# Half-width products in a triangular inversion, and a last tile that leaves in three pieces

## The chip, the cores and the metric

The program runs on one core of a Trainium2 chip, in one launch. The metric is the time of one execution on the device in microseconds (us). The kernel before took 2224.36 us, the median of three runs.

## The reference

One inference step of a two-layer decoder trunk, for a prompt of 2048 tokens of width 1024 and for 8 short samples of 8 tokens. Layer 0 mixes tokens with a gated DeltaNet of 6 heads, layer 1 with a short gated convolution. Both layers have memory attention beside the mixer, a gate, an output projection and a residual add; a final RMSNorm ends the trunk. The change touches two places of it, the solve in the delta rule and the end:

```python
A = jnp.tril(jnp.einsum('bnhid,bnhjd->bnhij', kb, k) * decay, -1)
rhs = jnp.concatenate([kb * jnp.exp(G)[..., None], v * beta[..., None]], axis=-1)
wu = lax.linalg.triangular_solve(A + jnp.eye(C, dtype=A.dtype), rhs, left_side=True,
                                 lower=True, unit_diagonal=True)
...
x = x + br @ w_out[i].astype(x.dtype)
...
y = rmsnorm(x, final_norm_g)
```

## The kernel before

**The order of the work.** The kernel is written as many small generators ("jobs"). A planner, `Flow` (lines 143 to 230), runs them while it records the instructions: it keeps a clock for each engine from a table of costs and always goes on with the job of highest priority that is ready on PE's clock. The order of the instructions on each engine is what comes out of this, so a changed cost moves instructions everywhere behind it. On the chip every engine takes its instructions strictly in that order and waits on semaphores. `mm` (line 319) issues all matrix products, so they all show as L330; the vector, scalar and GpSimd instructions all show as L281.

**The tiles.** Activations lie as 4 tiles of 512 tokens, plus one tile of the 64 sample tokens. A projection of a tile by a weight block is 24 products: 8 blocks of the depth, three float16 partial products each, 512 columns wide (64 for the samples). They are named `psp<-ht,whl` in layer 0.

**The inversion.** In layer 0 each head and tile is an item with 4 chunks of 128 tokens (one of 64 for the samples). `wy_inv` (lines 1552 to 1636) inverts the unit lower triangular matrices of two chunks at a time, 128 by 128 each, by doubling: at level `li`, blocks of side `1 << li` are joined in pairs. It holds U, the transposed inverse so far, and L, both float16, in one buffer `UL` (profile name `ul`). A level has four steps:

- PE: `pq`, A16 by L, 2 products of 128 columns (one for each chunk).
- DVE: `qq`, `pq` times a mask of the level, 128x256 to float16.
- PE: `pu`, `qq` by U and U by `qq`, 4 products of 128 columns.
- ACT: one copy of all of `pu`, 128x512, back into `ul`.

There are 6 such levels (2 for the samples), 24 items with two inversions each, so 288 levels of the wide kind, and 12 of the narrow. At a level, though, only half of the columns of U and of L get new values; in `qq` the other half are columns of the identity. GpSimd (POOL) makes U's first value and the low part `Ml` of the matrix, and works at other things in the same phase: the gates' masks `gm`, the identity added in `dd`, `whl` (the low halves of the weights) and the powers `rk`, `rq` and `hr`. `qq`, `A16`, `Ml`, `gm` and `ee` share 12 buffers (`kqc`).

**The end.** In layer 1 `out_group` (lines 2052 to 2111) makes the output projection of the tiles in the order 0, 1, 2, samples, 3. Tile 3 is done in two units of 256 tokens. Each of a unit's 8 blocks loads its rows of the residual (`xo`), and `ev` adds the product to them on DVE. `final` (lines 2130 to 2144) takes the unit's RMSNorm through `row_scale` (line 644): squares on ACT, their sum over the 8 blocks one after the other on POOL, one product with ones (`rb`) on PE, a power on POOL, a second product that spreads the result over the partitions, and then for each block one DVE instruction, which writes `yt`, a buffer of 4, and one store.

Of the kernel before, what the change touches and what calls it, by code (L numbers as in the profile page):

```python
# [15 lines left out]
AF = mybir.ActivationFunctionType  # L16
ALU = mybir.AluOpType
# [4 lines left out]
P = 128  # L22
D = 1024
KB = 8
NT = 4
# [261 lines left out]
def hybrid_kernel(  # L287
# [107 lines left out]
    def gbank(name):  # L395
        return psum("bank", [P, 4, P], 8, name)
# [16 lines left out]
    def kq16(name):  # L413
        return gp.tile([P, 2, P], F16, tag="kq", name=name, bufs=NKQ)
# [322 lines left out]
    def half(name, w=UN):  # L737
        return k1(name).rearrange("p z f -> p (z f)")[:, :w]
# [661 lines left out]
    def rows(x, n, C):  # L1400
        return x[:n, :n].rearrange("p (o f) -> p o f", o=1).to_broadcast([n, C, n])
# [150 lines left out]
    def wy_inv(it, i):  # L1552

        n, hc = it.n, it.hc
        lv = 7 if n == P else 3
        yield from wait(it.M_ok[i])
        M = it.M[i]  # L1560
        G.tensor_tensor(M[:n, :hc, :n], M[:n, :hc, :n], rows(identKh, n, hc), op=ALU.add)
        yield
        yield from ulc.get()
        yield from kqc.get(2)
        A16 = kq16("A16")
        V.tensor_copy(A16[:n, :hc, :n], M[:n, :hc, :n])
        UL = gp.tile([P, 4, P], F16, tag="k1", name="ul", bufs=NK1)
        U, L = UL[:n, 0:2], UL[:n, 2:4]
        yield
        yield from gc_.get()  # L1570
        pq = gbank("pq")
        for z in range(hc):
            mm(pq[:n, z, :n], A16[:n, z, :n], identh[:n, :n])
        t = fl.cur.t
        G.tensor_tensor(U[:, :hc, :n], A16[:n, :hc, :n], rows(mask_u, n, hc), op=ALU.mult)
        fl.cur.t, fl.cur.eng = t, "PE"
        yield
        V.tensor_tensor(L[:, :hc, :n], pq[:n, :hc, :n], rows(masks[:, 0], n, hc), op=ALU.mult)
        gc_.put()
        yield  # L1580
        Ml = None
        for li in range(1, lv):
            yield from gc_.get()
            pq = gbank("pq")
            for z in range(hc):
                mm(pq[:n, z, :n], A16[:n, z, :n], L[:, z, :n])
            if Ml is None:
                t = fl.cur.t
                Ml = kq16("Ml")
                G.tensor_tensor(Ml[:n, :hc, :n], M[:n, :hc, :n], A16[:n, :hc, :n], op=ALU.subtract)  # L1590
                fl.cur.t, fl.cur.eng = t, "PE"
                Mc.put()
            yield
            yield from kqc.get()
            qq = kq16("qq")
            V.tensor_tensor(qq[:n, :hc, :n], pq[:n, :hc, :n], rows(masks[:, li], n, hc), op=ALU.mult)
            gc_.put()
            yield
            yield from gc_.get()
            pu = gbank("pu")  # L1600
            for z in range(hc):
                mm(pu[:n, z, :n], qq[:n, z, :n], U[:, z, :n])
            for z in range(hc):
                mm(pu[:n, 2 + z, :n], U[:, z, :n], qq[:n, z, :n])
            kqc.put()
            yield
            if hc == 2:
                A.activation(UL[:n, :, :n], pu[:n, :, :n], AF.Copy)
            else:
                A.activation(UL[:n, 0:4:2, :n], pu[:n, 0:4:2, :n], AF.Copy)  # L1610
            gc_.put()
            yield
        yield from gc_.get()
        pe = gbank("pe")
        for z in range(hc):
            mm(pe[:n, z, :n], A16[:n, z, :n], L[:, z, :n], start=True, stop=False)
            mm(pe[:n, z, :n], Ml[:n, z, :n], L[:, z, :n], start=False, stop=True)
        yield
        kqc.put(2)
        yield from kqc.get()  # L1620
        ee = kq16("ee")
        V.tensor_tensor(ee[:n, :hc, :n], rows(identKh, n, hc), pe[:n, :hc, :n], op=ALU.subtract)
        gc_.put()
        yield
        yield from uc.get()
        yield from gc_.get()
        pu = gbank("pu1")
        for z in range(hc):
            mm(pu[:n, z, :n], ee[:n, z, :n], U[:, z, :n])
        kqc.put()  # L1630
        yield
        it.u[i] = k1("u1")
        V.scalar_tensor_tensor(it.u[i][:n, :hc, :n], pu[:n, :hc, :n], 1.0 / MS, U[:, :hc, :n], op0=ALU.mult, op1=ALU.add)
        gc_.put()
        ulc.put()
        fl.set(it.u_ok[i])
# [415 lines left out]
    def out_group(l, src, src_s, consume):  # L2052
# [2 lines left out]
        units = [(t, slice(0, TOK if t < NT else NS)) for t in seqn]  # L2055
        if l == 1:
            i = seqn.index(NT - 1)
            units[i:i + 1] = [(NT - 1, slice(u * UN, (u + 1) * UN)) for u in range(2)]
        for i, (t, cs) in enumerate(units):
            N = cs.stop - cs.start  # L2060
            yield from wait(ready[l][t])
# [9 lines left out]
            for k in range(KB):  # L2071
                w = ws[k]
                yield from use(w)
                with fl.aside():
                    V.tensor_tensor(isc8[:, k:k + 1], w.inv, inv, op=ALU.mult)
                if N == TOK:
                    yield from pc.get()
                    xo = piece("xo")
                    landed = dma(xo, src[t, :, k])
                elif t < NT:  # L2080
                    yield from xhc.get()
                    xo = half("xo")
                    landed = dma(xo, src[t, :, k, cs])
                else:
                    xo = xos[:, k]
                xt.append(xo)
                yield from ppc.get()
                ps = pbank()
                yield from proj(ps[:, :N], w, hl[:, :, :, cs])
                if i + 1 == len(units):  # L2090
                    w.free()

                def ev(ps=ps, xo=xo, k=k, t=t, N=N, isc8=isc8, landed=landed, fs=fs):
                    yield until(landed)
                    V.scalar_tensor_tensor(xo, ps[:, :N], isc8[:, k:k + 1], xo, op0=ALU.mult, op1=ALU.add)
                    ppc.put()
                    fl.set(fs[k])
                    if t < NT and l == 0:
                        yield
                        dma(x1_sp[t, :, k], xo)  # L2100
                    yield 0

                fl.spawn(5, ev(), "xo")
# [25 lines left out]

    def final(t, cs, xt, fs):  # L2130
        N = cs.stop - cs.start
        rb = yield from row_scale(xt, fs, N, G, (tmpc0, tmp0))
        for k in range(KB):
            yield from tmpc.get()
            yt = tmp("yt", N)
            V.scalar_tensor_tensor(yt, xt[k], fg[:, k:k + 1], rb[:, :N], op0=ALU.mult, op1=ALU.mult)
            if t < NT:
                (pc if N == TOK else xhc).put()
            yield
            dma((y_o[t] if t < NT else ys_o)[:, k, cs], yt)  # L2140
            tmpc.put(1, 2500.0)
        gc_.put()
        if t == NT:
            pc.put()
# [158 lines left out]
```

## Time and profile before

| | |
|---|---|
| median of 3 runs | 2224.36 us (2221.85 to 2230.78) |
| the profiled execution, its own time | 2225.13 us |
| its span, first to last instruction | 2223.4 us |
| PE busy | 2147.2 us, 97% |
| DVE, ACT, POOL busy | 1488.9, 1120.7 and 714.3 us |
[...]

The busy time of PE counts each product from its start to the modelled end. Products are pipelined: the next one starts long before the one in front has ended. So what a product costs in a row of them is read from the distance of starts in the timeline, not from its own duration.

### The profile page before, as it was taken

What the parts mean: (1) busy time and instruction counts of PE and PEld (TensorE: products, weight loads), DVE (VectorE), ACT (ScalarE), POOL (GpSimd) and SP (SyncE); (2) the same over time, 40 slices, a digit from 0 to 9 for tenths busy, and PEclk for the clock granted to TensorE, in tenths of its full rate; (3) what the DMA queues carried; (4) which work ended last, traced back from release to release, by engine and by line L of the source; (5) the groups of instructions that cost most, each with busy time, mean ns of one, the idle gap of its engine ahead of it and who ended that gap; (6) DMA issues with size and microseconds to landing.
All of it is one profiled execution on the core that took longest, in us unless ns stands there. A gap on an engine that the chain in (4) does not pass through costs nothing.

```text
span 2223.4 us, 43011 instructions
## 1 busy us (share of the span) xinstructions
PE 2147.2 (97%) x16176; PEld 1298.0 (58%) x16176; DVE 1488.9 (67%) x4228; ACT 1120.7 (50%) x2952; POOL 714.3 (32%) x901
## 2 busy tenths in 40 slices
PE   6889989999999999999999999999999999999998
PEld 5467657667666666666555454455444456555457
DVE  6988887887889878777777566355342437675354
ACT  5757665566657656566566345134221226653221
POOL 5655334442434433433222335012110212201322
PEclk9989999999999999999999999999999999999999
DMA  4201020201122102002134443022010111223433
GB/s 134 64 13 37 16 49 9 55 30 27 39 70 41 50 6 46 31 6 69 56 102 143 142 152 114 15 68 80 31 54 10 53 49 58 69 72 129 129 112 118
DMA packets 113634, 141.50 MB, mean 64 GB/s; under 512 B 50193, under 2 KB 67857, under 8 KB 113425
## 3 DMA queue, kind: packets, MB, share of 16 engines
q1 hardware_dynamic: 113424, 138.75, 20.5%
q8 instruction: 127, 2.08, 0.4%
q14 instruction: 83, 0.67, 0.1%
HBM read 99.22 MB, written 39.49 MB: 62 GB/s over the span
## 4 chain that ended last, share of the span: by engine, by line
PE 58%; DVE 3%; ACT 1%; issue 1%; DMA 1%; POOL 0%; POOLq 0%; DVEq 0%; ACTq 0%
PE psp L330 49%; PE psA L330 2%; PE psc L334 1%; PE pu L330 1%; PE po L330 1%; PE psc L330 1%; PE rb L330 1%; DVE wmx L281 1%; PE pq L330 1%; PE pqk L330 0%; DVE amx L281 0%; PE pkk L330 0%; DMA wraw<-in_wo 0%; DVE apT L281 0%; PE po L334 0%
## 5 line engine op out<-in xcount | busy, mean ns | idle before, releaser
L330 PE MATMUL psp<-ht,whl 128*128 128x512 f16 x5376 | 1270.0, 380 | 0.0
L330 PEld LDWEIGHTS <-whl 128*128 128x128 f16 x9408 | 753.6, 98 | 650.1 <-issue 12.6
L281 POOL TENSOR_TENSOR whl<-wraw,whl 128x512 f16<-128x512 f32 x184 | 216.8, 1182 | 448.0 <-ACT whl L281 400.2
L330 PE MATMUL psp<-hl,whl 128*128 128x512 f16 (+1 forms) x1728 | 342.4, 357 | 0.0
L281 ACT ACTIVATE ul<-pu 128x512 f16<-128x512 f32 x300 | 168.3, 582 | 79.6 <-PE pu L330 76.8
L281 ACT ACTIVATE wraw<-wraw,wsc 128x512 f32<-128x512 f32 (+1 forms) x186 | 131.7, 712 | 76.3 <-DVE wsc L281 44.6
L281 DVE SCALAR_TENSOR_TENSOR cacc<-psp,cws,cacc 128x511 f32<-128x511 f32 (+2 forms) x216 | 159.4, 738 | 10.1 <-ACT cacc L281 9.8
L281 POOL TENSOR_TENSOR nsq<-nsq 128x512 f32<-128x512 f32 (+2 forms) x105 | 100.6, 960 | 194.3 <-ACT nsq L281 149.1
L281 DVE TENSOR_TENSOR qq<-pq,masks 128x256 f16<-128x256 f32 x300 | 118.0, 407 | 51.1 <-PE pq L330 49.2
L281 DVE TENSOR_REDUCE wmx<-wraw 128x1 f32<-128x1024 f32 (+1 forms) x93 | 111.5, 1201 | 31.6 <-DMA wraw<-in_wb 24.5
L281 ACT ACTIVATE wg<-psp,hisc 128x512 f32<-128x512 f32 x64 | 44.0, 687 | 171.6 <-PE psp L330 171.4
L281 ACT ACTIVATE nsq<-xo 128x512 f32<-128x512 f32 (+1 forms) x72 | 41.4, 580 | 150.8 <-DVE xo L281 86.8
L281 ACT ACTIVATE whl<-wraw 128x512 f16<-128x512 f32 x184 | 114.8, 626 | 2.7
L281 DVE SCALAR_TENSOR_TENSOR xo<-psp,isc,xo 128x512 f32<-128x512 f32 (+1 forms) x72 | 49.6, 688 | 95.2 <-PE psp L330 95.2
L281 DVE SCALAR_TENSOR_TENSOR wg<-wg,psp 128x512 f32<-128x512 f32 x64 | 43.6, 681 | 87.8 <-ACT wg L281 87.8
L330 PEld LDWEIGHTS <-A 128*128 128x128 f16 x792 | 69.4, 100 | 41.1 <-issue 10.4
L281 ACT ACTIVATE ape<-psc,amx,sa 128x256 f32<-128x256 f32 x128 | 70.8, 561 | 31.7 <-DVE amx L281 31.6
L330 PE MATMUL pu<-ul,qq 128*128 128x128 f16 (+1 forms) x588 | 81.8, 224 | 3.9 <-DVE qq L281 3.1
L330 PE MATMUL pq<-ul,A 128*128 128x128 f16 (+1 forms) x588 | 77.0, 224 | 4.6 <-ACT ul L281 2.6
L330 PE MATMUL pu<-qq,ul 128*128 128x128 f16 (+1 forms) x588 | 81.2, 223 | 0.0
L281 POOL TENSOR_TENSOR rk<-sse,mhalf 128x4 f32<-128x4 f32 (+1 forms) x30 | 27.6, 919 | 159.9 <-DVE sse L281 118.8
L281 DVE SCALAR_TENSOR_TENSOR raw<-psp,wisc,cg 128x512 f32<-128x512 f32 x24 | 18.0, 749 | 86.9 <-PE psp L330 86.8
(344 smaller groups left out, 3641.0 us busy)
## 6 DMA issues: line engine op xcount, KB each, us to landing
br_sp<-wg SPq DMA_DIRECT2D x64, 256.0 KB, 2.0
brl<-br_sp SPq DMA_DIRECT2D x64, 256.0 KB, 2.9
wraw<-in_wb SPq DMA_DIRECT2D x28, 512.0 KB, 3.5
wraw<-in_wa SPq DMA_DIRECT2D x24, 512.0 KB, 3.5
xk<-in_x SPq DMA_DIRECT2D x64, 128.0 KB, 2.9
wraw<-in_wo SPq DMA_DIRECT2D x16, 512.0 KB, 3.4
xo<-in_x SPq DMA_DIRECT2D x32, 256.0 KB, 3.5
x_sp<-xo SPq DMA_DIRECT2D x32, 256.0 KB, 2.4
```

The lines of the kernel that those rows point to most:

```text
L281: return f(out, *args, **kw)
L330: nc.tensor.matmul(out, lhsT=lhsT, rhs=rhs, start=start, stop=stop)
L334: nc.tensor.transpose(out, in_, ident)
```

## The change

In the inversion, the products of a level are made for the half of the columns that changes, 64 instead of 128 (32 instead of 64 for the samples); DVE masks half as many elements; ACT brings back the two halves in two instructions of 128x128, and the other halves of `ul` stay as they are. The half of `qq` that is a piece of the identity is written by a new POOL instruction (`unit`), ahead of the level: for the first one before the loop, for each later one right behind the `pu` products of the level before. The columns that change lie in runs of `1 << li` elements, with equal gaps.

At the end, tile 3 is done in units of 256, 128 and 128 tokens. The second and the third share the rows that are loaded for both. The last unit sums its squares with 8 products on PE instead of on POOL. `final` scales the rows in place and stores them from there; a row's buffer comes free 2.5 us (on the planner's clock) behind the store.

```diff
--- before.py
+++ after.py
@@ -1579,35 +1579,59 @@
         gc_.put()
         yield
         Ml = None
+
+        def halves(x, li):
+
+            v = x[:, :, :n].rearrange("p z (b h s) -> p z b h s", h=2, s=1 << li)
+            return v[:, :, :, 0], v[:, :, :, 1]
+
+        idh = identh[:n, :n].rearrange("p (o f) -> p o f", o=1)
+
+        def unit(li):
+
+            qq = kq16("qq")
+            i2 = halves(idh, li)[1].to_broadcast([n, hc, n >> (li + 1), 1 << li])
+            G.tensor_tensor(halves(qq[:n], li)[1][:, :hc], i2, i2, op=ALU.mult)
+            return qq
+
+        yield from kqc.get()
+        qq = unit(1)
+        fl.cur.t, fl.cur.eng = t, "PE"
         for li in range(1, lv):
+            nb = n >> (li + 1)
+            first, second = halves(L, li), halves(U, li)
+            qf = halves(qq[:n], li)[0]
             yield from gc_.get()
-            pq = gbank("pq")
+            pq = gbank("pq").rearrange("p c (b s) -> p c b s", s=1 << li)
             for z in range(hc):
-                mm(pq[:n, z, :n], A16[:n, z, :n], L[:, z, :n])
+                mm(pq[:n, z, :nb], A16[:n, z, :n], first[0][:, z])
+            t = fl.cur.t
             if Ml is None:
-                t = fl.cur.t
                 Ml = kq16("Ml")
                 G.tensor_tensor(Ml[:n, :hc, :n], M[:n, :hc, :n], A16[:n, :hc, :n], op=ALU.subtract)
-                fl.cur.t, fl.cur.eng = t, "PE"
                 Mc.put()
-            yield
-            yield from kqc.get()
-            qq = kq16("qq")
-            V.tensor_tensor(qq[:n, :hc, :n], pq[:n, :hc, :n], rows(masks[:, li], n, hc), op=ALU.mult)
+            fl.cur.t, fl.cur.eng = t, "PE"
+            yield
+            mask = halves(masks[:n, li:li + 1], li)[0].to_broadcast([n, hc, nb, 1 << li])
+            V.tensor_tensor(qf[:, :hc], pq[:n, :hc, :nb], mask, op=ALU.mult)
             gc_.put()
             yield
+
             yield from gc_.get()
-            pu = gbank("pu")
+            pu = gbank("pu").rearrange("p c (b s) -> p c b s", s=1 << li)
             for z in range(hc):
-                mm(pu[:n, z, :n], qq[:n, z, :n], U[:, z, :n])
+                mm(pu[:n, z, :nb], qq[:n, z, :n], second[1][:, z])
             for z in range(hc):
-                mm(pu[:n, 2 + z, :n], U[:, z, :n], qq[:n, z, :n])
+                mm(pu[:n, 2 + z, :nb], U[:, z, :n], qf[:, z])
+            t = fl.cur.t
             kqc.put()
-            yield
-            if hc == 2:
-                A.activation(UL[:n, :, :n], pu[:n, :, :n], AF.Copy)
-            else:
-                A.activation(UL[:n, 0:4:2, :n], pu[:n, 0:4:2, :n], AF.Copy)
+            if li + 1 < lv:
+                yield from kqc.get()
+                qq = unit(li + 1)
+            fl.cur.t, fl.cur.eng = t, "PE"
+            yield
+            A.activation(second[1][:, :hc], pu[:n, :hc, :nb], AF.Copy)
+            A.activation(first[0][:, :hc], pu[:n, 2:2 + hc, :nb], AF.Copy)
             gc_.put()
             yield
         yield from gc_.get()
@@ -2055,7 +2079,8 @@
         units = [(t, slice(0, TOK if t < NT else NS)) for t in seqn]
         if l == 1:
             i = seqn.index(NT - 1)
-            units[i:i + 1] = [(NT - 1, slice(u * UN, (u + 1) * UN)) for u in range(2)]
+            units[i:i + 1] = [(NT - 1, slice(a, b)) for a, b in ((0, UN), (UN, UN + P), (UN + P, TOK))]
+            rows_in = []
         for i, (t, cs) in enumerate(units):
             N = cs.stop - cs.start
             yield from wait(ready[l][t])
@@ -2078,9 +2103,11 @@
                     xo = piece("xo")
                     landed = dma(xo, src[t, :, k])
                 elif t < NT:
-                    yield from xhc.get()
-                    xo = half("xo")
-                    landed = dma(xo, src[t, :, k, cs])
+                    if cs.start <= UN:
+                        yield from xhc.get()
+                        rows_in.append(half("xo"))
+                        landed = dma(rows_in[-1], src[t, :, k, cs.start:cs.start + UN])
+                    xo = rows_in[KB * (cs.start >= UN) + k][:, cs.start % UN:cs.start % UN + N]
                 else:
                     xo = xos[:, k]
                 xt.append(xo)
@@ -2129,16 +2156,14 @@
 
     def final(t, cs, xt, fs):
         N = cs.stop - cs.start
-        rb = yield from row_scale(xt, fs, N, G, (tmpc0, tmp0))
+        last = cs.start == TOK - P
+        rb = yield from row_scale(xt, fs, N, None if last else G, (tmpc0, tmp0))
         for k in range(KB):
-            yield from tmpc.get()
-            yt = tmp("yt", N)
-            V.scalar_tensor_tensor(yt, xt[k], fg[:, k:k + 1], rb[:, :N], op0=ALU.mult, op1=ALU.mult)
-            if t < NT:
-                (pc if N == TOK else xhc).put()
-            yield
-            dma((y_o[t] if t < NT else ys_o)[:, k, cs], yt)
-            tmpc.put(1, 2500.0)
+            V.scalar_tensor_tensor(xt[k], xt[k], fg[:, k:k + 1], rb[:, :N], op0=ALU.mult, op1=ALU.mult)
+            yield
+            dma((y_o[t] if t < NT else ys_o)[:, k, cs], xt[k])
+            if t < NT and N != P:
+                (pc if N == TOK else xhc).put(1, 2500.0)
         gc_.put()
         if t == NT:
             pc.put()
```

Some rows of the order of instructions, before and after.

PE in layer 0, where the first inversion makes its first `pq` (`A` is A16, `ul` holds U and L; a piece of the difference):

```order
 L330 MATMUL psp<-ht,whl 128x512
 L330 LDWEIGHTS A_1568
-L330 MATMUL pq<-ul,A_1568 128x128
+L330 MATMUL pq<-ul,A_1568 128x64
 L330 LDWEIGHTS A_1568
-L330 MATMUL pq<-ul,A_1568 128x128
+L330 MATMUL pq<-ul,A_1568 128x64
```

Each product keeps its own load of a full weight; its moving side is half as wide.

POOL in layer 0, at the first item behind a samples' item. Before (`rq` is a power, `dd` gets the identity added):

```order
L281 TENSOR_TENSOR M<-M,identKh 128x256 x2
L281 TENSOR_TENSOR ul<-A_5211,mask_u 128x256
L281 TENSOR_TENSOR ul<-A_5218,mask_u 128x256
L281 TENSOR_TENSOR rq<-ssq,mhalf 128x4
L281 TENSOR_TENSOR dd<-dd,ident 128x256 x2
L281 TENSOR_TENSOR Ml<-M,A_5211 128x256
L281 TENSOR_TENSOR Ml<-M,A_5218 128x256
L281 TENSOR_TENSOR gm<-sLh,ghl 128x256 x4
L281 TENSOR_TENSOR whl<-wraw,whl 128x512
```

With the change:

```order
L281 TENSOR_TENSOR ul<-A_5302,mask_u 128x256
L281 TENSOR_TENSOR qq<-identh 128x32x4
L281 TENSOR_TENSOR qq<-identh 128x64x2
L281 TENSOR_TENSOR Ml<-M,A_5302 128x256
L281 TENSOR_TENSOR qq<-identh 128x32x4
L281 TENSOR_TENSOR qq<-identh 128x16x8
L281 TENSOR_TENSOR rq<-ssq,mhalf 128x4
L281 TENSOR_TENSOR dd<-dd,ident 128x256 x2
L281 TENSOR_TENSOR qq<-identh 128x16x8
L281 TENSOR_TENSOR whl<-wraw,whl 128x512
L281 TENSOR_TENSOR gm<-sLh,ghl 128x256 x2
L281 TENSOR_TENSOR qq<-identh 128x8x16 x2
```

The identity pieces of the levels now stand between POOL's other instructions, some of them behind `rq` and two `dd`, or behind a `whl` and two `gm`.

DVE at the end of the program. Before (`isc` is a scale, `nm` the mean of the squares):

```order
L281 SCALAR_TENSOR_TENSOR xo<-psp,isc_29297,xo 128x256
L281 TENSOR_TENSOR isc_29297<-winv,binv 128x1
L281 SCALAR_TENSOR_TENSOR xo<-psp,isc_29297,xo 128x256 x2
L281 TENSOR_SCALAR nm<-rb 128x2
L281 SCALAR_TENSOR_TENSOR yt<-xo,fg,rb 128x256 x8
```

With the change:

```order
L281 SCALAR_TENSOR_TENSOR xo<-psp,isc_30150,xo 128x128
L281 TENSOR_TENSOR isc_30150<-winv,binv 128x1
L281 SCALAR_TENSOR_TENSOR xo<-psp,isc_30150,xo 128x128 x2
L281 TENSOR_REDUCE nm<-rb 128x1
L281 TENSOR_SCALAR nm<-nm 128x1
L281 SCALAR_TENSOR_TENSOR xo<-xo,fg,rb 128x128 x8
```

The same steps stand there in half the width, with one small reduction more, and the scaled rows go back to where they came from.

## Rows read from the trace of the kernel before

**Rows 1.** Busy time by stretch: from:to, length, PE, PEld, DVE, ACT, POOL, clock, DMA.

```profile
110.00:1060.00 950.00, 921.54 (x7680) 632.29 (x7679) 775.55 (x2494) 596.06 (x1816) 381.96 (x529) 0.99 0.14 35
1060.00:2168.00 1108.00, 1097.46 (x7554) 570.90 (x7554) 606.41 (x1431) 448.78 (x933) 255.79 (x259) 1.00 0.25 82
2168.00:2223.40 55.40, 45.22 (x418) 39.89 (x414) 24.31 (x69) 6.73 (x18) 12.93 (x20) 0.94 0.37 119
```

**Rows 2.** PE's waits, 110 to 1060 us: waiter, awaited, us, times, longest.

```profile
PE pu L330 <- DVE qq L281: 3.1, 6, 1.2
```

**Rows 3.** Groups by line and form, PE, 110 to 1060 us: busy us, mean ns, idle.

```profile
L330 PE MATMUL pu<-ul,qq 128*128 128x128 f16 x576 | 79.2, 224 | 3.9 <-DVE qq L281 3.1
...
L330 PE MATMUL pq<-ul,A 128*128 128x128 f16 x576 | 74.5, 224 | 4.6 <-ACT ul L281 2.6 <-DVE ssq L281 1.2 <-issue 0.4
```

**Rows 4.** Timeline, 702.66 to 703.74 us: start, length, engine, instruction, count.

```profile
702.66 0.22 PE L330 MATMUL pe<-ul,A 128*128 128x128 f16 x1
...
702.83 0.80 PEld L330 LDWEIGHTS <-whl 128*128 128x128 f16 x24
702.88 0.86 PE L330 MATMUL psp<-hs_t,whl 128*128 128x64 f16 x24
```

**Rows 5.** Groups by line and form, PE, 110 to 1060 us, two other products.

```profile
L330 PE MATMUL psp<-hs_t,whl 128*128 128x64 f16 x672 | 28.5, 193 | 0.6 <-issue 0.6
...
L330 PE MATMUL psp<-hm,whl 128*128 128x128 f16 x96 | 6.2, 219 | 0.0
```

**Rows 6.** Groups by line and form, DVE, whole span.

```profile
L281 DVE TENSOR_TENSOR qq<-pq,masks 128x256 f16<-128x256 f32 x288 | 115.7, 415 | 48.1 <-PE pq L330 46.4 <-PE psp L330 0.4
...
L281 DVE SCALAR_TENSOR_TENSOR S<-S,eGl,psA 128x128 f32<-128x128 f32 x90 | 30.7, 341 | 24.3 <-PE psA L330 16.6 <-PE pq L330 3.3 <-ACT hm L281 1.3
...
L281 DVE TENSOR_TENSOR o<-qs,psA 128x128 f32<-128x128 f32 x90 | 25.0, 278 | 0.0
```

**Rows 7.** Groups by line and form, ACT, whole span.

```profile
L281 ACT ACTIVATE ul<-pu 128x512 f16<-128x512 f32 x288 | 165.6, 595 | 76.5 <-PE pu L330 73.7 <-PE psp L330 1.6
...
L281 ACT ACTIVATE kd<-pk 128x128 f32<-128x128 f32 x96 | 25.2, 282 | 3.6 <-PE pk L334 3.6
```

**Rows 8.** Groups by line and form, POOL, 110 to 1060 us.

```profile
L281 POOL TENSOR_TENSOR dd<-dd,ident 128x256 f32<-128x256 f32 x48 | 35.1, 751 | 0.0
...
L281 POOL TENSOR_TENSOR ul<-A,mask_u 128x256 f16<-128x256 f16 x48 | 32.4, 685 | 25.9 <-DVE A L281 24.6 <-POOL dd L281 0.8 <-PE pq L330 0.2
...
L281 POOL TENSOR_TENSOR rq<-ssq,mhalf 128x4 f32<-128x4 f32 x22 | 23.0, 1045 | 15.4 <-DVE ssq L281 15.2
...
L281 POOL TENSOR_TENSOR ul<-A,mask_u 64x64 f16<-64x64 f16 x6 | 1.8, 298 | 4.2 <-DVE A L281 4.2
```

**Rows 9.** Timeline, one level of an inversion, 701.38 to 703.89 us.

```profile
701.38 0.27 PE L330 MATMUL pu<-qq,ul 128*128 128x128 f16 x2
...
701.76 0.60 ACT L281 ACTIVATE ul<-pu 128x512 f16<-128x512 f32 x1 [1.45 <-PE pu L330]
...
702.55 0.28 PE L330 MATMUL pq<-ul,A 128*128 128x128 f16 x2
...
703.14 0.41 DVE L281 TENSOR_TENSOR qq<-pq,masks 128x256 f16<-128x256 f32 x1
...
703.61 0.28 PE L330 MATMUL pu<-ul,qq 128*128 128x128 f16 x2
```

**Rows 10.** Timeline, after the last product, 2211.9 to 2223.4 us.

```profile
2211.94 0.48 DVE L281 SCALAR_TENSOR_TENSOR xo<-psp,isc,xo 128x256 f32<-128x256 f32 x1 [2.14 <-PE psp L330]
...
2213.08 0.72 POOL L281 TENSOR_TENSOR nsq<-nsq 128x256 f32<-128x256 f32 x1 [1.90 <-ACT nsq L281]
...
2213.85 0.61 PE L330 MATMUL rb<-ones,nsq 128*128 128x1 f32 x4 [1.95 <-POOL nsq L281]
...
2216.75 4.22 SPq L344 DMA_DIRECT2D out_y<-yt  x8
```

**Rows 11.** Timeline, PE alone, the last unit's products.

```profile
2199.29 12.61 PE L330 MATMUL psp<-hl,whl 128*128 128x256 f16 x114
```

## The prediction

> **What bounds the kernel now.** I read the busy time by stretch first. From 110 to 1060 us, where nearly all of the inversions run, PE is busy for 921.5 of 950 us, DVE for 775.6, ACT for 596.1 and POOL for 382.0; from 1060 to 2168 us PE is busy for 1097.5 of 1108 us [rows 1]. So PE's queue is what sets the time, and an edit is worth what it takes out of that queue, less the holes that it opens there. The reader should then look at PE's waits: in 300 levels the product `pu` stood idle for the mask on DVE 6 times, 3.1 us in all [rows 2]. The chain of a level (PE, DVE, PE, ACT) is long, but projections of other items fill it. A shorter chain is therefore worth little here, and a shorter product is worth its full spacing.
>
> **Part 1: 64 columns for 128 on PE.** There are 288 wide levels with 2 `pq` and 4 `pu` products each, 1728 in all; the groups show 576 for each of the three forms, of which two stand here [rows 3]. Their 224 ns is a duration in a pipeline and not a price. The price is the distance of starts. Four `pe` products of 128 columns start from 702.66 us on (the first is shown), and the row behind them starts at 702.88 us [rows 4]: 0.22 / 4 = 55 ns each. In that row 24 products of 64 columns, each with its own load of a 128x128 weight, take 0.86 us from the first start to the last end; one alone has 193 ns [rows 5]. So (860 - 193) / 23 = 29 ns each. The saving is 26 ns x 1728 = **45 us**. From above: the groups give 6.2 us / 96 = 65 ns for 128 columns [rows 5], and 65 - 29 = 36 ns would make 62 us; but that figure has tails of bursts in it. From below the end is nothing, if something else than columns paces these products. I take 45, the row of a dense train. The 36 products of the samples' inversions are left at nothing: they are already at 64 columns, and too few.
>
> What might pace them is the weight load. The trace shows 24 loads in 0.80 us beside the 24 products [rows 4], 33 ns each. [...]
>
> **Part 2: the mask on DVE and the copies on ACT.** The mask takes 415 ns for 256 elements; the nearest instruction with 128 elements from PSUM takes 278 ns [rows 6]. That is 137 ns x 288 = 39 us less on DVE, beside PE's work. One ACT copy of 595 ns becomes two of 128 elements; the nearest such copy has 282 ns [rows 7], so 564 for 595, 9 us less in all. Both lie beside PE: I cost them at nothing, and what hides them is the projections that fill PE between `pu`, `pq` and `pu`. If that cover were gone, a level's chain would still be shorter by 0.17 us, so nothing is lost here.
>
> **Part 3: the identity pieces on POOL.** 288 new instructions of 128 elements, float16. Between 298 ns for 64 and 685 ns for 256 elements [rows 8] the slope is 2.0 ns, so 427 ns each and 123 us in all: POOL goes from 382 to 505 us in a phase of some 905 us, 56%. This adds a wait: `pu` loads `qq` as its weight and now needs POOL as well as DVE, and DVE's product into the same buffer may itself stand behind the POOL piece, with the scans' R and S queued behind it on DVE. The piece is asked for one level ahead. A level in the trace goes from `pu` at 701.26 us (its second pair starts at 701.38) over the copy at 701.76, `pq` at 702.55 and the mask at 703.14 to the next `pu` at 703.61 [rows 9]: 2.35 us. That is the cover. In the order with the change, some pieces stand behind `rq` and two `dd`: 1.045 + 2 x 0.751 = 2.55 us [rows 8], and with their own 0.43 they are 0.6 us late if nothing of that was done before. One such place in each of the 24 items would cost 15 us. From above: 58 of the 288 pieces stand behind over 2 us of other POOL work; 0.6 us each makes 35 us. From below nothing, because POOL would still idle for 44% and the level shown is a quick one; below nothing is excluded by the added work. Nearest is the row of the same product waiting for DVE, which is busier: 3.1 us [rows 2]. I take **8 us**, between that row and the 15.
>
> **Part 4: the last tile.** 192 products of 256 columns become 384 of 128. The train of 114 takes 12.61 us [rows 11], at most 111 ns each; two of 55 cost the same. The last unit's sum by 8 products with ones instead of one adds 7; four took 0.61 us [rows 10], so +1.0 us in PE's queue. Behind the last product, `xo` starts at 2211.94 us and the first store at 2216.75 [rows 10]. The POOL add of that chain (from 2213.08 to the product with ones at 2213.85, with the wait in front some 0.9 us) goes, and steps such as `xo` shrink from 0.48 to 0.34 us (an instruction with 128 elements, 341 ns [rows 6]); the added reduction costs about 0.2. I take 1.5 us less. The 8 stores take SP 4.22 us to issue [rows 10], and that stays. Sum: **-0.5 us**, between -3 and +1. Writing in place takes no more buffers of 4, and rows are held until their store is out; the 8 more stores of the middle unit go out while PE makes the last one. I cost that at nothing: PE's queue is full there, and 4 of the 12 row buffers are free for the next tile; without that cover a late row would hold a PSUM bank and stop PE.
>
> **Sum.** The profiled execution took 2225.1 us (its span is 2223.4), 0.8 above the median of the runs. 2225.1 - 45 + 8 - 0.5 = 2187.6; against the median **2187 us**.
>
> **Rivals.**
> - *The forecast's chain with a free POOL.* The pieces are always early, and DVE's 39 us closes some holes: 950 - 921.5 = 28.5 us of idle PE, of which I give 8 us back. 2187 - 8 - 8 = **2171 us**. For it: POOL's 44% of idle time. Against: the bunches in its order. Chance 0.13.
> - *The strided reads cost more.* At the first two levels the 64 columns lie in runs of 4 and 8 bytes, so they touch the same stretch of the buffer as 128 did. If that paced the product, two levels of six would save nothing, 15 us: **2202 us**. No row here has such a read. Chance 0.08. [...]
> - *POOL is often late.* 35 us for 8: **2214 us**, half of it over the bound of no change. Chance 0.10.
> - *Weight loads pace the products.* Nothing saved: 2187 + 45 = **2232 us**, within the bound of no change. The row of 24 loads speaks against it. Chance 0.02. [...]
> - *POOL paces the levels, and the kernel is slower.* Place: the two inversions of an item side by side, 144 pairs of levels. In a pair POOL has two pieces (0.85 us) and, where `rq` and two `dd` or their like fall between, 2.55 us more: 3.40 against 2.35, so PE stops for 1.05 us. At 45 / 1.05 = 43 such pairs the gain is gone; at all 58 places counted above it is 61 us, so 2187 - 8 + 61 = **2240 us**. Against it: many of the 58 stand at the start of an inversion, where time is long, and PE now hardly waits for a busier DVE. Chance 0.05.
> - That it does not do what it says: the order shows the halved forms, so this has no chance of its own.
>
> **How the numbers follow.** Forecast 0.62. About 0.5%, 11 us, is what a measurement of this kernel can tell from no change, so the bound is 2213 us. Faster: 0.62 + 0.13 + 0.08 + half of 0.10 = 0.88. Same: 0.05 + 0.02 = 0.07. Slower: 0.05. The range, 2168 to 2208, holds the forecast, the stride and most of the free POOL, some 0.8 together.
>
> **What would show it.** In the profile after: the three forms at 128x64, with starts 29 ns apart in a train; `qq` on DVE near 280 ns, two copies near 280 ns on ACT; 288 POOL pieces near 430 ns. The phase should end 37 us earlier, and nothing should move between there and the last tile. PE's waits for `pu` should name POOL or a mask behind it with some 8 us. A row of PE waits on `qq` over 30 us, or starts of 45 ns or more apart at the levels with short runs, would make the prediction wrong, and so would a first phase that is as long as before with larger holes.

## The result, and the profile after

The changed kernel took 2200.11 us (median of 4 runs, 2195.47 to 2208.19); the kernel before, in the same session, 2223.88 us (2221.85 to 2230.78). The ratio is 0.9892 with an interval of 0.9852 to 0.9931. In a second session it was 2205.32 against 2224.36 us, 0.9915 (0.990 to 0.993). So it is faster by some 19 to 24 us. Forecast were 37 us less and 2187; the time lies within the range, 13 to 18 us above the forecast.

The profiled execution took 2208.19 us (its span is 2206.4), the longest of the four; that of the second session took 2200.55 us (span 2198.7), the shortest of its six. Busy time by stretch, same columns as in [rows 1]:

```profile
110.00:1060.00 950.00, 907.68 (x7808) 605.62 (x7806) 761.07 (x2516) 564.39 (x2138) 502.81 (x834) 0.97 0.14 36
1060.00:2168.00 1108.00, 1097.90 (x7603) 576.23 (x7599) 608.77 (x1442) 443.70 (x920) 256.33 (x263) 1.00 0.26 85
```

PE is now idle for 42.3 us of the first stretch (28.5 before), POOL has 121 us more to do (382 to 503), and the granted clock of the stretch is 0.97, not 0.99. The second stretch is as it was. The groups by line and form in the first stretch answer to [rows 3, 6 and 7]:

```profile
L281 ACT ACTIVATE ul<-pu 128x128 f16<-128x128 f32 x576 | 120.2, 283 | 66.8 <-PE pu L330 61.7 <-PE psp L330 2.2 <-PE pq L330 2.2
L281 POOL TENSOR_TENSOR qq<-identh 128x128 f16<-128x128 f16 x288 | 115.4, 419 | 21.8 <-PE pu L330 8.5 <-PE pd L330 6.2 <-DVE dd L281 1.4
L281 DVE TENSOR_TENSOR qq<-pq,masks 128x128 f16<-128x128 f32 x288 | 75.9, 283 | 35.1 <-PE pq L330 34.4
...
L330 PE MATMUL pu<-ul,qq 128*128 128x64 f16 x576 | 58.7, 196 | 8.3 <-POOL qq L281 3.2 <-DVE qq L281 3.0 <-POOL M L281 1.5
...
L330 PE MATMUL pq<-ul,A 128*128 128x64 f16 x576 | 56.9, 197 | 7.2 <-ACT ul L281 6.8
```

A train of these products on the timeline (start, length, instruction, count):

```profile
704.92 0.22 PE L330 MATMUL pu<-ul,qq 128*128 128x64 f16 x2
...
704.98 0.22 PE L330 MATMUL pu<-qq,ul 128*128 128x64 f16 x2
...
705.04 0.22 PE L330 MATMUL pu<-ul,qq 128*128 128x64 f16 x2
...
705.10 0.22 PE L330 MATMUL pu<-qq,ul 128*128 128x64 f16 x2
```

Each pair starts 0.06 us after the one ahead of it: 30 ns a product, each with a weight load of its own (eight loads stand beside the eight products, from 704.87 to 705.20 us). Over all six levels the median distance of starts between two such products of one kind is 29 ns (56 before), with 28 and 32 ns at the tenth and ninetieth percentile. At the two levels whose columns lie in runs of 4 and 8 bytes it is 31 ns.

What PE waits for in the first stretch (waiter, awaited, us, times, longest; `S` and `qs` are tiles of the scan over the chunks, which stands behind the inversion), before:

```profile
PE psA L330 <- ACT vh L281: 4.3, 1, 4.3
PE pu L330 <- DVE qq L281: 3.1, 6, 1.2
PE pq L330 <- ACT ul L281: 2.6, 5, 1.6
...
PE psA L330 <- DVE qs L281: 1.6, 5, 0.6
...
PE psA L330 <- DVE S L281: 1.4, 4, 0.7
```

and after:

```profile
PE pq L330 <- ACT ul L281: 6.8, 8, 3.0
PE psA L330 <- DVE S L281: 5.7, 6, 2.1
PE psA L330 <- DVE qs L281: 3.6, 5, 2.0
PE pu L330 <- POOL qq L281: 3.2, 6, 0.8
PE pu L330 <- DVE qq L281: 3.0, 4, 1.5
```

Summed over all rows of this view: 26.6 us before (DVE 17.4, ACT 8.0, POOL 0) and 40.8 after (DVE 24.7, ACT 10.5, POOL 4.7). In the profile of the second session it is 43.4 (25.5, 12.0, 4.9).

The granted clock of TensorE shows a second loss: its mean over the span is 0.983, for 0.989 before. In four stretches of the trace after (from:to, length, the engines as above, clock third from the end):

```profile
422.00:425.50 3.50, 1.48 (x16) 1.04 (x15) 3.47 (x7) 0.51 (x3) 3.50 (x6) 0.99 0.25 64
425.60:432.30 6.70, 6.70 (x19) 2.95 (x18) 2.76 (x11) 0.65 (x3) 2.98 (x7) 0.50 0.11 42
706.00:708.80 2.80, 0.77 (x6) 0.58 (x5) 0.15 (x1) 0.53 (x2) 0.00 (x0) 0.99 0.04 1
708.80:715.60 6.80, 6.02 (x24) 3.18 (x24) 5.07 (x22) 3.53 (x12) 2.65 (x7) 0.50 0.01 1
```

PE has work for less than half of the first and third stretch; in the stretch behind each, the clock is 0.50 of full speed. In the first of the two, six `psp` products of 512 columns take 2.55 us from the first start to the start behind them (429.14 to 431.69 us), and 1.30 us at full clock (952.01 to 953.31 us). Such stretches add up to 27 us between 110 and 1060 us before, and to 58 us after (41 in the second session's profile).

The tail, from the last sum of squares on:

```profile
2197.32 0.35 DVE L281 SCALAR_TENSOR_TENSOR xo<-psp,isc,xo 128x128 f32<-128x128 f32 x1 [1.37 <-PE psp L330]
...
2198.07 0.38 PE L330 MATMUL rb<-ones,nsq 128*128 128x1 f32 x2 [0.79 <-ACT nsq L281]
...
2200.63 3.65 SPq L344 DMA_DIRECT2D out_y<-xo  x8
```

The POOL add of [rows 10] is gone; from the last `psp` product to the end it is 9.1 us, not 11.5. But PE's queue ahead of it is longer. The last tile's products begin and end, before (the end is the row of [rows 11], at 2211.90 us):

```profile
2168.23 2.02 PE L330 MATMUL psp<-hl,whl 128*128 128x256 f16 x17
```

and after:

```profile
2150.19 2.02 PE L330 MATMUL psp<-hl,whl 128*128 128x256 f16 x17
...
2196.95 0.33 PE L330 MATMUL psp<-hl,whl 128*128 128x128 f16 x3
```

That is 43.7 us before and 47.1 after, so the whole last tile takes 1 us more than before.

### The profile page after: what moved, and what is told of

Read it like the earlier page. It is cut to its first block, busy times and chain, and to the rows that moved or that the text cites. A ratio compares the mean times of both kernels' runs of the same rounds, so it can differ in the third digit from the quotient of the medians.

```text
span 2206.4 us, 44527 instructions
## 1 busy us (share of the span) xinstructions
PE 2117.5 (96%) x16382; PEld 1264.7 (57%) x16382; DVE 1468.0 (67%) x4254; ACT 1082.8 (49%) x3260; POOL 828.2 (38%) x1202
## 4 chain that ended last, share of the span: by engine, by line
PE 52%; DVE 2%; issue 0%; DMA 0%; ACT 0%; POOL 0%; POOLq 0%; DVEq 0%; SPq 0%; ACTq 0%
PE psp L330 46%; PE psc L334 1%; PE po L330 1%; PE psc L330 1%; PE rb L330 1%; PE po L334 0%; PE psA L330 0%; DVE amx L281 0%; DMA xo<-x_sp 0%; DVE xo L281 0%; PE psT L330 0%; PE spo L330 0%; DVE nhs L281 0%; PE pam L330 0%; POOL nsq L281 0%
## 5 line engine op out<-in xcount | busy, mean ns | idle before, releaser
L330 PE MATMUL psp<-hl,whl 128*128 128x512 f16 (+2 forms) x1920 | 343.8, 337 | 0.0
L281 POOL TENSOR_TENSOR nsq<-nsq 128x512 f32<-128x512 f32 (+3 forms) x105 | 96.5, 921 | 184.5 <-ACT nsq L281 158.4
L281 ACT ACTIVATE ul<-pu 128x128 f16<-128x128 f32 x600 | 123.4, 279 | 68.9 <-PE pu L330 63.9
L281 DVE TENSOR_REDUCE wmx<-wraw 128x1 f32<-128x1024 f32 (+1 forms) x93 | 111.6, 1201 | 25.6 <-DMA wraw<-in_wb 21.9
L281 POOL TENSOR_TENSOR qq<-identh 128x128 f16<-128x128 f16 x300 | 118.2, 412 | 21.8 <-PE pu L330 8.5
L281 DVE SCALAR_TENSOR_TENSOR xo<-psp,isc,xo 128x512 f32<-128x512 f32 (+2 forms) x80 | 51.3, 642 | 109.2 <-PE psp L330 105.4
L281 ACT ACTIVATE nsq<-xo 128x512 f32<-128x512 f32 (+2 forms) x80 | 43.6, 545 | 157.4 <-DVE xo L281 103.9
L281 DVE SCALAR_TENSOR_TENSOR wg<-wg,psp 128x512 f32<-128x512 f32 x64 | 43.7, 682 | 87.6 <-ACT wg L281 87.5
L281 DVE TENSOR_TENSOR qq<-pq,masks 128x128 f16<-128x128 f32 x300 | 78.0, 278 | 35.3 <-PE pq L330 34.5
L330 PEld LDWEIGHTS <-A 128*128 128x128 f16 (+1 forms) x792 | 65.3, 101 | 45.0 <-issue 17.4
L330 PE MATMUL pu<-ul,qq 128*128 128x64 f16 x588 | 61.0, 196 | 8.4 <-POOL qq L281 3.2
L281 ACT ACTIVATE jk<-o 128x128 f32<-128x128 f32 x96 | 30.1, 313 | 77.6 <-DVE o L281 72.2
```

The costliest lines, as they stand in the source:

```text
L281: return f(out, *args, **kw)
L330: nc.tensor.matmul(out, lhsT=lhsT, rhs=rhs, start=start, stop=stop)
```

## The experiments

All kernels but that of the last tile alone are the changed kernel with one edit; except for the old prices and the two kernels with one part each, they keep its order on every engine. The edits are shown in part; `...` marks what is left out. Ratios are to the kernel before, run on the same chip in the same rounds. The table collects them; the clock is the mean over the runs of a kernel, the waits are PE's between 110 and 1060 us, summed as above.

| kernel | ratio (interval) | clock | waits: DVE, ACT, POOL; all |
|---|---|---|---|
| before | 1 | 0.988 to 0.990 | 17.4, 8.0, 0; 26.6 |
| changed (first session) | 0.9892 (0.9852, 0.9931) | 0.985 | 24.7, 10.5, 4.7; 40.8 |
| changed (second session) | 0.9915 (0.990, 0.993) | 0.985 | 25.5, 12.0, 4.9; 43.4 |
| 128 columns | 1.0026 (1.0013, 1.004) | 0.989 | 22.7, 9.3, 4.6; 39.6 |
| no pieces | 0.9897 (0.9876, 0.9917) | 0.983 | 31.6, 8.9, 0; 40.7 |
| pieces twice | 0.997 (0.9957, 0.9982) | 0.983 | 26.4, 6.2, 20.7; 55.0 |
| no second `pu` | 0.9859 (0.9844, 0.9873) | 0.983 | 32.7, 8.7, 5.1; 46.8 |
| old prices | 0.9938 (0.9924, 0.9952) | 0.988 | 30.0, 6.0, 6.8; 46.1 |
| half the mask | 0.9889 (0.9867, 0.991) | 0.984 | 24.9, 12.2, 3.4; 41.7 |
| holes filled | 0.9936 (0.9916, 0.9956) | 0.988 | 20.1, 8.4, 1.8; 33.5 |
| same work elsewhere | 0.9976 (0.9967, 0.9986) | 0.989 | 23.7, 13.5, 3.1; 41.4 |
| six holes | 0.9901 (0.9884, 0.9918) | 0.987 | 21.9, 7.7, 4.7; 35.7 |
| inversion alone | 0.9902 (0.9885, 0.9919) | 0.984 | 23.1, 12.4, 4.6; 42.0 |
| last tile alone | 0.9994 (0.9984, 1.0003) | 0.989 | 17.3, 9.4, 0; 27.4 |

**128 columns in the new order.**

```diff
-                mm(pq[:n, z, :nb], A16[:n, z, :n], first[0][:, z])
+                mm(pq[:n, z, :2 * nb], A16[:n, z, :n], L[:, z, :n].rearrange("p (b h s) -> p h b s", h=2, s=1 << li), price=n // 2)
...
```

(both `pu` products likewise, and the first copy on ACT reads the half that is wanted; `price` is what the planner is told.)

> The changed kernel with its order and all other instructions as they are, but the 1728 products pq and pu of the inversion are 128 columns wide again (the unneeded half is computed into the other 64 columns of the bank and never read). PE's work is larger by the 45 us that the traces before and after differ by. Three theories of why the change gave some 24 us in the median and not 37 or 45. Clock theory (the columns' 45 us come off in full, and a part of it is given back because PE, with the same waits and less work between them, is granted half clock more often: 58 us between 110 and 1060 us in the trace after, 27 in the one before): the stretches at half clock shrink towards 30 us again, so the time rises by less than 45, to about 2225 to 2235. Pool theory (the identity pieces come late and PE waits for them at every width): the holes stay or are hidden by the wider products, 2235 to 2245. Order theory (the planner's other order costs some 15 us): the whole 45 us come on top, 2245, that is 20 above the kernel before.

Measured: 0.0111 above the changed kernel, 25 us (30 by the first session's ratio), within the first theory's range. Against the kernel before it has the same products of the inversion on PE and is 6 us slower, with 39.6 us of waits for 26.6 at the same clock. So the new order with its pieces costs some 6 us even where the products are as long as before; and taking 45 us out of PE's queue in that order brought only 25 to 30. Of the rest, the clock explains part: from 0.989 to 0.985 is 0.004 x 2205 = 9 us of PE's time, an estimate from above, since it counts PE as always busy and its work as longer by as much as the clock is lower (2.55 for 1.30 us at 0.50). Three rows of its waits, to set beside those of the changed kernel above:

```profile
PE pq L332 <- ACT ul L281: 6.3, 6, 2.3
PE psA L332 <- DVE S L281: 5.3, 6, 1.8
...
PE psA L332 <- DVE qs L281: 3.7, 5, 2.0
```

They are as long as with products of half the width.

**No pieces, and pieces twice.**

```diff
-            G.tensor_tensor(halves(qq[:n], li)[1][:, :hc], i2, i2, op=ALU.mult)
...
+            fl.op("POOL", 150.0 + 1.66 * count(i2), qq, [i2, i2])
...
```

> The changed kernel in its own order on every engine, without the 288 identity pieces on POOL: four buffers hold an identity that is written once with the masks, and the masked products of every level go to their first 64 columns, so the identity stands in the wrong columns at most levels and the output is not the reference's. POOL loses 115 us of work, and no product waits for a piece. Pool theory: PE's waits for qq on POOL (3.2 us) and what follows from them go, 2187 to 2192. Clock theory: 0 to 6 us less than the changed kernel, 2194 to 2200, with as much half clock as before or a little less.

```diff
             G.tensor_tensor(halves(qq[:n], li)[1][:, :hc], i2, i2, op=ALU.mult)
+            nc.gpsimd.tensor_tensor(halves(qq[:n], li)[1][:, :hc], i2, i2, op=ALU.mult)
```

> The changed kernel in its own order, but each identity piece is written twice in a row by POOL, 115 us more of POOL's work (618 instead of 503 us between 110 and 1060 us). Pool theory: a piece that is on the path now is later by another 419 ns at each of 288 places of which a part is exposed, at least 12 us more, 2212 or above. Clock theory: the pieces are taken between other work, 0 to 6 us more, 2200 to 2206.

PE's waits in the kernel without pieces:

```profile
PE pq L330 <- ACT ul L281: 8.5, 4, 4.8
PE psA L330 <- DVE S L281: 8.0, 5, 3.8
PE pu L330 <- DVE qq L281: 3.9, 5, 2.0
```

and with the pieces twice:

```profile
PE pu L330 <- POOL qq L1595: 15.1, 13, 3.9
PE pq L330 <- ACT ul L281: 6.0, 6, 2.3
```

Without pieces, POOL's waits are gone, DVE's have grown from 25 to 32 us, and the time can't be told from that of the changed kernel (0.9897; the intervals overlap). Taking off 115 us of POOL's work was worth nothing that shows, though a gain of some 4 us, as by the second session's ratio, isn't excluded: where POOL had ended a wait last, something else now ends it. Doubled, the pieces cost 0.0055, 12 us, as the pool theory had it, with 20.7 us of waits for POOL. So POOL stands near an edge: its present load is covered by the other waits, and 115 us more is not.

**Without the second `pu` product.**

```diff
-                mm(pu[:n, 2 + z, :nb], U[:, z, :n], qf[:, z])
+                mm(pu[:n, 2 + z, :nb], U[:, z, :n], qf[:, z], issue=False)
...
```

> The changed kernel in its own order without the second product of every update (pu from U and the masked half, 576 products of 64 columns with their weight loads, 29 ns each, 16.7 us of PE's work); the lower half then takes a copy of the upper one's result, so the output is not the reference's. If a saving on PE arrives in full in this phase: 2183. Clock theory: a part of it goes into waits and into more stretches at half clock, so 4 to 12 us arrive, 2188 to 2196, and the half clock between 110 and 1060 us is at least the 58 us of the changed kernel.

16.7 us less on PE gave 0.0056, 12 us, by the second session's ratio and 7 by the first's. Waits rose to 46.8 us, the clock fell to 0.983, and the stretches at 0.50 add up to 68 us in its profile: the next saving in this queue is again paid only in part, as the clock theory had it.

**Old prices.** The products stay at 64 columns; the planner counts 128.

```diff
-                mm(pq[:n, z, :nb], A16[:n, z, :n], first[0][:, z])
+                mm(pq[:n, z, :nb], A16[:n, z, :n], first[0][:, z], price=n)
...
```

(both `pu` products likewise.)

> The changed kernel, but the planner is told that each product pq and pu of the inversion is as long as in the kernel before, so it sets another order; the products themselves are 64 columns wide. Order theory (the 128 columns in the changed kernel's order came out 6 us above the kernel before, and that is the new order's doing): with the old prices PE's waits are fewer, 3 to 8 us less than the changed kernel, a ratio of 0.985 to 0.988. If the order is not it (the pieces on POOL and DVE's and ACT's waits are, and these go with any order): 0.989 to 0.992.

Slower than the changed kernel by 0.0023, 5 us, above both ranges, with more waits (46.1) at a higher clock. The expected gain is missing, so old prices are no remedy. The difference is hardly larger than the two intervals, but the rows of the waits are others:

```profile
PE pam L332 <- DVE wmx L281: 6.1, 5, 2.8
...
PE psA L332 <- DVE S L281: 2.8, 3, 2.2
PE pq L332 <- ACT ul L281: 2.6, 6, 0.7
...
PE psA L332 <- DVE qs L281: 1.9, 6, 0.5
```

The last three sum to 7.3 us here, and to 16.1 and 18.8 us in the two profiles of the changed kernel, which has the same short products, copies and pieces. Which of PE's waits are long goes with the order.

**Half the mask on DVE.**

```diff
-            V.tensor_tensor(qf[:, :hc], pq[:n, :hc, :nb], mask, op=ALU.mult)
...
+            nc.vector.tensor_tensor(qf[:, :1], pq[:n, :1, :nb], mask[:, :1], op=ALU.mult)
...
```

> The changed kernel in its own order, but the mask of qq on DVE is done for one of the two heads of a pair and both heads' products read that one, so the output is not the reference's; PE, ACT and POOL do the same instructions as in the changed kernel. The traces show PE waiting for DVE 17.4 us between 110 and 1060 us before the change, 24.7 and 25.5 after it. Theory that DVE comes late now because PE has 45 us less to cover it with: DVE's work falls by some 20 to 30 us, PE's waits for DVE to 15 to 20 us, and the time by 4 to 9 us, a ratio of 0.9875 to 0.990 to the kernel before (the changed kernel: 0.9915). If those waits are set by chains through several engines rather than by how much DVE has to do, or if the order is their cause: DVE's waits stay at 23 us or more and the time within 3 us of the changed kernel, 0.990 to 0.993.

DVE's work in the phase fell from 761 to 742 us, PE's waits for DVE stayed at 24.9, and the interval of the time overlaps the changed kernel's. The ratio, 0.9889, lies in the first theory's range, but the waits by which it was to come about didn't fall; its six runs lie 17 us apart, from 2195.15 us at a clock of 0.988 to 2212.19 at 0.982. The waits speak for the second theory: those that name DVE are not set by how much DVE has to do.

**The holes filled, the same work elsewhere, and six holes.**

```diff
+    def fill(out, start=True):
+        ns = FILL.get(calls[0], 0)
...
+            for _ in range(int(ns / (0.43 * cols))):
+                nc.tensor.matmul(out, lhsT=identh[:, :out.shape[0]], rhs=identh[:, :cols], start=True, stop=True)
```

`FILL` holds the product in program order and the nanoseconds; the three kernels differ in this table alone. (The 714 products went to 20 places.)

> The changed kernel in its own order, with 714 extra products of an identity (some 30 us of PE's work at full clock) that nobody reads: they go to the output of the product that waits, just ahead of it, at 21 places between 64 and 1040 us where the trace after shows PE without work for 0.9 to 3.3 us, as many as fill the hole but for 0.25 us. Clock theory: with the holes filled the granted clock stays up, the half clock between 110 and 1060 us falls from 58 to 35 us or less, and the time falls though PE has 30 us more to do: 2185 to 2197, a ratio to the kernel before of 0.982 to 0.987. If the half clock is only a sign that travels with the waits, or is not set off by such holes: no gain, and up to 30 us more where a hole is smaller in other executions, a ratio of 0.989 to 1.003.

> The changed kernel in its own order with the same 30 us of extra identity products as in the kernel that fills the holes, in as many portions, but each some 25 to 50 products later in the program (in one place further on), ahead of the first product of another tile. If the granted clock is kept up by filling the holes: here the holes stay, the half clock between 110 and 1060 us stays at 45 us or more, and the extra work costs 22 to 31 us, a ratio of 1.000 to 1.006 (the filled holes gave 0.9936, the changed kernel in the same rounds as later runs 0.9915). If any 30 us of extra products raise the clock as well, or fill as much waiting: the half clock falls to 35 us here too, and the ratio is 0.992 to 0.997.

> The changed kernel in its own order with extra identity products in six holes only, those ahead of the half clock at 251, 303, 425, 709 and 1036 us whose filling took effect, six tenths of each hole, 6 us of work in all. Clock theory: some 15 to 25 us of half clock less than the changed kernel and 1 to 2 us of holes filled, so 6 us of work come back: a ratio of 0.986 to 0.990, 0 to 4 us below the changed kernel. If such portions help only when all holes are filled: 2 to 6 us above it.

Busy time between 110 and 1060 us with the holes filled, and with the work elsewhere:

```profile
110.00:1060.00 950.00, 914.71 (x8373) 624.52 (x8373) 752.16 (x2503) 557.47 (x2122) 499.86 (x832) 0.98 0.14 35
```

```profile
110.00:1060.00 950.00, 907.06 (x8398) 615.47 (x8397) 743.84 (x2479) 555.33 (x2111) 497.76 (x830) 0.98 0.13 35
```

With the holes filled, the stretches at 0.50 fell from 58 (41) to 31 us, as expected, but the time did not fall: it is 0.0021, 5 us, above the changed kernel. 30 us of work cost 5: 33.5 us of waits are left of 43, and the mean clock is back at 0.988; these two make up some 10 and 7 us (0.003 x 2205, the estimate above) of the 25 that came back, and the rest isn't accounted for. Put elsewhere, the same work cost 0.0061, 14 us, between the two ranges; the waits stayed at 41 us, the stretches at 0.50 add up to 41 us, and the mean clock over the runs rose just as much, to 0.989, which the first theory had not expected. So the clock does not hang on these holes alone: 30 us of added work in PE's queue raised it here, in the holes or not. The 9 us between the two kernels are about the 8 us of waits that one fills and the other does not. Six holes alone gave 0.9901, 3 us below the changed kernel, but within its interval, and the stretches at 0.50 were 48 us in its profile, not 15 to 25 less than the changed kernel's 58 or 41. So that a filled hole prevents the half clock behind it isn't shown.

**Each part alone.** The inversion's edit with the old last tile, and the last tile's pieces with the old inversion.

> The change of the inversion alone; the last tile leaves in two halves as in the kernel before. If nearly all of the gain is the inversion's: the changed kernel's time and some 2.4 us, a ratio to the kernel before of 0.988 to 0.993. If the last tile's pieces carry a good part: above 0.994.

> The change of the last tile alone; the inversion's products, masks and updates are 128 columns wide as in the kernel before. The end after the last psp product is shorter by 2.4 us in the trace after: a ratio of 0.998 to 1.000. If the pieces of 128 columns save products or bring the stores forward by more than that: below 0.997.

Measured: 0.9902 (0.9885 to 0.9919) and 0.9994 (0.9984 to 1.0003). The gain is the inversion's; the last tile's pieces are worth 1 us, by an interval that includes no change. In every kernel with the new last tile its products and their waits take 2.8 to 4.4 us longer and the end behind them is 2.1 to 2.9 us shorter than in the two kernels with the old one.

**The changed kernel again.**

> The changed kernel itself, for a ratio on the same chip and in the same rounds as the two kernels with extra products. Clock theory and all others: 0.987 to 0.993, a half clock of 50 to 65 us between 110 and 1060 us.

Its six runs show the price of the clock without any edit. The furthest apart are 2200.55 us at 0.988 and 2210.78 at 0.983, 10 us for 0.005, and 0.005 x 2205 = 11 us by the same estimate; but 2203.12 us at 0.987 and 2205.95 at 0.983 are only 3 us apart. Its profile, at 0.988, has the same products and nearly the same waits as the first one, and 41 instead of 58 us at 0.50. The expectation of 50 to 65 us was missed there, so how much a single execution loses to the clock varies, here by some 3 to 10 us.

## Why the prediction was right, and where its sum was not

**The bound** was read rightly: PE's queue in the first stretch sets the time, and the second stretch is unchanged (PE busy 1097.9 for 1097.5 us).

**Part 1** held: in a train the products start 29 to 31 ns apart for 56, at every level. If the products of the two profiled traces are added up, each at the usual distance of its kind to the next, the queue is shorter by 45 us. The rival of strided reads fell with that: 2 ns a product at two of the six levels are some 1 us. The rival of weight loads fell too: the train above has a product every 30 ns, with a load each. A load of 128 columns lasts 100 ns in the trace (busy us, mean ns):

```profile
L330 PEld LDWEIGHTS <-qq 128*128 128x128 f16 x576 | 46.2, 100 | 29.0 <-POOL qq L281 7.3 <-issue 3.6 <-POOL M L281 1.6
```

That is the duration of a load and not the distance of two loads. The row of 24 loads in 0.80 us, which are of a kind that lasts 98 ns in the mean before the change, shows that the loads overlap, as the products do.

**Part 2** failed: the step "I cost them at nothing, and what hides them is the projections that fill PE". The instructions came out as priced (283 ns on DVE and on ACT), but PE's waits for DVE and ACT together, 25.4 us before, became 35.2 and 37.5. The rows that grew most are `pq` for the copy on ACT (2.6 to 6.8) and the scan's `psA` for S and qs on DVE (3.0 to 9.3), the latter work that the change does not touch. The first of them is less clear than it looks, for the kernel with the old inversion and the new last tile has it too:

```profile
PE pq L330 <- ACT ul L281: 6.1, 6, 4.7
```

Its rows of S and qs are 3.5 us, near the 3.0 before the change. Less work on DVE did not shrink PE's waits for DVE. In the new order the waits for DVE and ACT are nearly as large with 128 columns (32.0 us, with 9.0 for S and qs), and with the short products in the order of the old prices S and qs are 4.7 us. So the rows of the scan go with the order that the planner wrote for the shorter products, and not with the products' width. No order with fewer waits in all is shown: under the old prices others took their place.

**Part 3** had nearly the right size in the wrong place. POOL's pieces take 419 ns for 427, POOL has 503 us for 505, and POOL ends 4.7 to 4.9 us of PE's waits, for 8. But without the pieces the time is the same within the intervals, so that the size came out is luck; the 6 us by which the new order with 128 columns is above the kernel before belong to the order as a whole. The rivals that rest on POOL fell: waits on `qq` are 6.2 us, not over 30. With the pieces twice POOL is the one that is late.

**Part 4**: -0.5 forecast, from +1.0 in PE's queue and -1.5 behind it. In the trace both are larger, +3.4 and -2.4, so the tile took 1.0 us more (0.4 in the second session's profile); the last tile alone gave 0.0006 (1 us) in its runs. The stores took 3.65 us to issue, not an unchanged 4.22; the added reduction takes 0.17 us, for about 0.2.

**Missing from the sum** was the granted clock: 0.985 in the mean for 0.988 to 0.990, some 8 us, an estimate with PE counted as always busy. With it and the waits the two profiles add up, as an estimate from the distances of starts over the whole span: -45 on products, +11 to +15 of waits at full clock and +14 to +18 of added length and waiting at the half clock (a hole at the edge of such a stretch can be put to either), in sum about -16; the spans differ by 17.0. In the second session's profile the waits are +15 to +17 and the half clock +5 to +6, which makes about -24, against 24.7.

**What would show it**: the phase should have ended 37 us earlier, and nothing should have moved between there and the last tile. The last product of an inversion starts at 1031.5 us (1028.0 in the second session) for 1054.8, so 23 to 27 earlier; from there to the last tile it took 5 us (2 us) more than before. With the last tile's 1.0 (0.4) that makes the 17 (25) us between the spans. The rival of a free POOL, 2171, fell with the holes: they grew.

**The range** held by luck in part. The time came out near the 2202 us of the strided reads, for which the range had been drawn that far, and those cost some 1 us; waits for DVE and ACT and the clock, which brought it there, had no term in the sum.

**Open**: from the kernel with 128 columns to the changed one, the ratios give 25 to 30 us, and 45 less the clock's 9 and 1 to 4 us of waits is 32 to 35. The difference is about what separates two executions of one kernel, and wasn't narrowed down. Why the clock is lower with the shorter products is open too.

## What to carry to other kernels

The shortened products gave their whole spacing back in PE's full queue here (29 ns for 56, 45 us in all), but only some 19 to 24 us of it arrived in the time: the rest went into waits, which came with the new order at either width of the products, and into clock. So price the saving by the distance of starts, and then the new idle time: add up the waits by engine before and after (26.6 and 40.8 us here), and the stretches at 0.50 of the clock (27 and 58 us). That an engine ended a wait last did not make it the cost here: POOL ended 4.7 us of PE's waits, yet taking its pieces away gave nothing that shows (0.9897, for 0.9892 and 0.9915), and only doubling them (0.997, 12 us) showed how near its edge it was.

## What the runs showed of the hardware that was not expected

In one and the same order the mean granted clock of TensorE was 0.983 without the second `pu`, 0.983 to 0.985 with the changed kernel's products, 0.987 with 6 us of useless products, and 0.988 to 0.989 with 128 columns or with 30 us of useless products, wherever they stood. It differed from execution to execution of one program by 0.005 in the changed kernel, with times 3 to 10 us apart, and by 0.008 in the kernel with half the mask. 30 us of useless products cost 5 us in holes and 14 us elsewhere.

A load of 128 columns takes 100 ns, and yet products with a load each start 29 ns apart. Products whose operands skip every second run of 4 or 8 bytes start 31 ns apart, for 29 with runs of 16 bytes and more.
